# One gate and one product per tile, with hand-counted semaphores in one critical section (SwiGLU, 8192 x 8192, fp32)

## Chip, cores and metric

One core of one Trainium2 chip. The metric is the device time of one execution in microseconds (us). "Span" is the length of the profiled execution, which is about 1.8 us shorter than the timed one. A transfer "lands" when its completion is signalled (the packet records put that about 0.3 us before the semaphores do), and "stands in line" while an earlier transfer of its queue is still under way. A packet is one piece of a transfer in the DMA records.

## The reference

```python
def reference(x):                      # x: 8192 x 8192 float32
    a, b = np.split(x, 2, axis=-1)
    return a * (b / (1 + np.exp(-b)))  # 8192 x 4096
```

Each element is read once and each result written once: 268.4 MB in, 134.2 MB out, hardly any arithmetic.

## The kernel before

A tile holds two rows of x on each of 128 partitions (64 KB each); there are 32 tiles and three buffers. Loads go out from the sync engine, the first 30 stores from GpSimd, the last three (tile 30, and the two halves of tile 31) again from the sync engine. The framework derives all waits.

```python
    def swiglu(i, k, c0=0, cw=half):               # one row k of tile i
        xt = tiles[i]
        b = xt[:, k * M + half + c0 : k * M + half + c0 + cw]
        nc.scalar.activation(out=b, in_=b, func=_SILU)
        nc.vector.tensor_mul(out=xt[:, k * half + c0 : ...], in0=xt[:, k * M + c0 : ...], in1=b)   # (cut)

    for i in range(BUFS):
        load(i)
    for i in range(last):                          # last = 31
        for k in range(R):                         # R = 2
            swiglu(i, k)
        if i == last - 1:
            swiglu(last, 0)
        store(i)
        ...                                        # load(i + 3); tile 31 in two halves
    store(last, 0, half)
    for c0 in range(0, half, half // 2):
        swiglu(last, 1, c0, half // 2)
    store(last, half, half)
```

## Time and profile before

| | before |
|---|---|
| time, median | 936.34 us in the first three runs, 935.93 in the six that stand beside the change |
| span of the profiled run | 934.3 us |
| DMA share of the two data queues | 99.8% |
| first data packet / end of the last one (packet records of the trace) | 1.76 us / 932.76 us |
| busy: vector engine, scalar engine | 30%, 25% |

The lines behind the shares are in the prediction, and so is what follows from them. This is the list of instructions of the framework's last line; columns are the queue, the instruction, its count, duration in ns (least, median, most), and first and last start:

```profile
L106 POOLq DRAIN  x3: 40/101/32876, 871.2 to 934.0; - x3
```

GpSimd's queue (POOL) begins a drain at 871.2 us, right after issuing its last store, and it lasts 32.9 us, until 904.1. The last GpSimd store has landed at 902.5 by the packet records. So this drain, an instruction that holds GpSimd's queue, ended 1.6 us after the last of its stores had landed, and it lies wholly beside other transfers.

### The profile page before, as it was taken

How to read it: one execution, taken by the hardware profiler on the slowest of the kernel's cores; microseconds unless marked ns; L12 is line 12 of the kernel's file. 1: busy time of each engine (PE TensorE's matmuls, PEld its weight loads, DVE VectorE, ACT ScalarE, POOL GpSimd, SP SyncE). 2: the span in 40 equal slices, each digit the busy share in tenths (PEclk: the TensorE clock that was granted, in tenths of full speed). 3: DMA queues.
4: the chain of work that ended last, by engine and by line, in shares of the span. 5: the costliest groups of instructions: out<-in, count | busy, mean ns of one | idle time of the engine just before them, and what ended most of it. 6: DMA issues, size and time to landing. Idle time of an engine off the chain costs nothing.

```text
span 934.3 us, 400 instructions
## 1 busy us (share of the span) xinstructions
DVE 283.3 (30%) x65; ACT 229.4 (25%) x66; POOL 16.3 (2%) x34
## 2 busy tenths in 40 slices
DVE  0333312333113332133321333213333133331252
ACT  0323330233311333113331133311333203332041
POOL 0000000000000000000000000000000000000000
DMA  9999999999999999999999999999999999999998
GB/s 404 404 449 426 425 448 424 436 429 446 428 422 441 432 446 424 446 415 453 428 421 456 415 452 421 427 450 415 442 428 441 429 435 428 438 450 414 437 432 383
DMA packets 9507, 402.68 MB, mean 431 GB/s; under 512 B 1056, under 2 KB 1056, under 8 KB 1056
## 3 DMA queue, kind: packets, MB, share of 16 engines
q1 hardware_dynamic: 5184, 276.83, 68.6%
q0 software_dynamic: 4320, 125.83, 31.2%
q14 instruction: 3, 0.02, 0.0%
HBM read 268.44 MB, written 134.22 MB: 431 GB/s over the span
## 4 chain that ended last, share of the span: by engine, by line
DMA 84%; DVE 10%; ACT 4%; issue 1%; DVEq 0%; SPq 0%; ACTq 0%
DMA out_dram<-xt 43%; DMA xt<-in_x_dram 40%; DVE xt L51 10%; ACT xt L50 4%; DVEq L106 0%; SPq L43 0%; ACTq L50 0%; DVEq L51 0%
## 5 line engine op out<-in xcount | busy, mean ns | idle before, releaser
L51 DVE TENSOR_TENSOR xt<-xt 128x4096 f32<-128x4096 f32 (+1 forms) x65 | 283.3, 4359 | 636.9 <-ACT xt L50 633.7
L50 ACT ACTIVATE xt<-xt 128x4096 f32<-128x4096 f32 (+1 forms) x65 | 228.1, 3556 | 687.3 <-DMA xt<-in_x_dram 687.3
L58 POOL DMA_DIRECT2D out_dram<-xt x30 | 16.1, 537 | 854.8 <-DVE xt L51 854.8
L50 ACT ACT_TABLE_LOAD x1 | 1.3, 1283 | 0.7 <-PEq L95 0.7
L95 POOL MEMSET const-float32-0.0<- 128x1 f32 x1 | 0.1, 99 | 0.2 <-issue 0.2
L95 POOL MEMSET const-bfloat16-1.0<- 128x1 bf16 x1 | 0.1, 102 | 0.0
L95 POOL MEMSET const-float32-1.0<- 128x1 f32 x1 | 0.1, 99 | 0.0
L95 POOL MEMSET const-uint8-127<- 128x1 uint8 x1 | 0.1, 99 | 0.0
## 6 DMA issues: line engine op xcount, KB each, us to landing
out_dram<-xt POOLq DMA_DIRECT2D x30, 4096.0 KB, 40.5
xt<-in_x_dram SPq DMA_DIRECT2D x2, 4096.0 KB, 26.4
out_dram<-xt SPq DMA_DIRECT2D x1, 4096.0 KB, 23.8
out_dram<-xt SPq DMA_DIRECT2D x2, 2048.0 KB, 14.5
xt<-in_x_dram SPq DMA_DIRECT2D x31, 33.5
```

The source lines that it names most:

```text
L50: nc.scalar.activation(out=b, in_=b, func=_SILU)
L51: nc.vector.tensor_mul(out=xt[:, k * half + c0 : k * half + c0 + cw], in0=xt[:, k * M + c0 : k * M + c0 + cw], in1=b,)
L58: (nc.gpsimd if i < last - 1 else nc.sync).dma_start(out=ov[i * P : (i + 1) * P, c0 : c0 + cw], in_=tiles[i][:, c0 : c0 + cw])
L95: nc = _bacc.Bacc("TRN2", target_bir_lowering=False, num_devices=1)
```

## The change

The intent is to have fewer instructions and no derived waits: one gate and one product per tile (tiles 1 to 30), and semaphores counted by hand, inside one critical section (a stretch of the program into which the framework puts no waits of its own). Cut to its core:

```diff
-    pool = ctx.enter_context(tc.tile_pool(name="sbuf", bufs=BUFS))
-    ctx.enter_context(tc.manual_schedule())
+    slots = [pool.tile([P, R * M], x.dtype, name=f"slot{s}") for s in range(BUFS)]
+    load_sem, store_sem = ...   # one per slot; and last_sem, gate_sem, prod_sem, end_sem
     def load(i, ...):
+        if i >= BUFS:
+            nc.sync.wait_ge(store_sem[s], 16 * (i // BUFS))
         nc.sync.dma_start(...)
+            .then_inc(last_sem if c0 else load_sem[s], 16)
     def swiglu(i, k0=0, k1=R, c0=0, cw=half):      # rows k0..k1 in one access pattern
+        nc.scalar.wait_ge(load_sem[s], 16 * (i // BUFS + 1))
         nc.scalar.activation(out=b, in_=b, func=_SILU).then_inc(gate_sem, 1)
+        nc.vector.wait_ge(gate_sem, counts["gate"])
         nc.vector.tensor_mul(...).then_inc(prod_sem, 1)
     def store(i, eng, ...):
+        eng.wait_ge(prod_sem, counts["prod"])
         inst = eng.dma_start(...)                   # then_inc(store_sem[s]) or, last three, end_sem
-    ... loop
+    with tc.tile_critical():
+        ... the same loop; tile 0 still in two rows
+        if i == last - 1:
+            swiglu(last, 0, 1)                     # counted before ...
+        store(i, ...)                              # ... the store of tile 30 is written
+        nc.sync.wait_ge(store_sem[(last - 2) % BUFS], 16 * ((last - 2) // BUFS + 1))
+        nc.sync.wait_ge(end_sem, 16 * counts["end"])
```

More of the change, by code (lines that the diff above doesn't have):

```diff
@@ L33 @@
     last = ntiles - 1
-    pool = ctx.enter_context(tc.tile_pool(name="sbuf", bufs=BUFS))
-    ctx.enter_context(tc.manual_schedule())
-    tiles = {}
-    def load(i, rows=None):
-        if i not in tiles:
-            tiles[i] = pool.tile([P, R * M], x.dtype, name="xt")
-        lo, hi = (0, R) if rows is None else rows
-        nc.sync.dma_start(
-            out=tiles[i][:, lo * M : hi * M], in_=xv[i * P : (i + 1) * P, lo * M : hi * M]
-        )
-    def swiglu(i, k, c0=0, cw=half):
-        xt = tiles[i]
-        b = xt[:, k * M + half + c0 : k * M + half + c0 + cw]
-        nc.scalar.activation(out=b, in_=b, func=_SILU)
-        nc.vector.tensor_mul(
-            out=xt[:, k * half + c0 : k * half + c0 + cw],
-            in0=xt[:, k * M + c0 : k * M + c0 + cw],
-            in1=b,
-        )
@@ L57, in store @@
-    def store(i, c0=0, cw=R * half):
-        (nc.gpsimd if i < last - 1 else nc.sync).dma_start(
-            out=ov[i * P : (i + 1) * P, c0 : c0 + cw], in_=tiles[i][:, c0 : c0 + cw]
-        )
-    for i in range(BUFS):
-        load(i)
-    for i in range(last):
-        for k in range(R):
-            swiglu(i, k)
-        if i == last - 1:
-            swiglu(last, 0)
-        store(i)
-        nxt = i + BUFS
-        if nxt < last:
-            load(nxt)
-        elif nxt == last:
-            load(last, (0, 1))
-            load(last, (1, 2))
@@ L77 @@
-    store(last, 0, half)
-    for c0 in range(0, half, half // 2):
-        swiglu(last, 1, c0, half // 2)
-    store(last, half, half)
+    pool = ctx.enter_context(tc.tile_pool(name="sbuf", bufs=1))
+    slots = [pool.tile([P, R * M], x.dtype, name=f"slot{s}") for s in range(BUFS)]
+    load_sem = [tc.alloc_semaphore(f"load{s}") for s in range(BUFS)]
+    store_sem = [tc.alloc_semaphore(f"store{s}") for s in range(BUFS)]
+    last_sem = tc.alloc_semaphore("last")
+    gate_sem = tc.alloc_semaphore("gate")
@@ new lines, with load, rows @@
+    prod_sem = tc.alloc_semaphore("prod")
+    end_sem = tc.alloc_semaphore("end")
+    def load(i, c0=0, cw=R * M):
+        s = i % BUFS
+        if i >= BUFS:
+            nc.sync.wait_ge(store_sem[s], 16 * (i // BUFS))
+        nc.sync.dma_start(
+            out=slots[s][:, c0 : c0 + cw], in_=xv[i * P : (i + 1) * P, c0 : c0 + cw]
+        ).then_inc(last_sem if c0 else load_sem[s], 16)
+    counts = {"gate": 0, "prod": 0, "end": 0}
+    def rows(ap, k0, k1, pitch, c0, cw):
+        return ap[:, k0 * pitch : k1 * pitch].rearrange("p (r w) -> p r w", w=pitch)[
+            :, :, c0 : c0 + cw
+        ]
@@ new lines, in swiglu @@
+    def swiglu(i, k0=0, k1=R, c0=0, cw=half):
+        s = i % BUFS
+        xt = slots[s]
+        b = rows(xt, k0, k1, M, half + c0, cw)
+        if i == last and k0:
+            nc.scalar.wait_ge(last_sem, 16)
+        else:
+            nc.scalar.wait_ge(load_sem[s], 16 * (i // BUFS + 1))
+        nc.scalar.activation(out=b, in_=b, func=_SILU).then_inc(gate_sem, 1)
+        counts["gate"] += 1
+        if k0:
+            nc.vector.wait_ge(prod_sem, counts["prod"])
+        nc.vector.wait_ge(gate_sem, counts["gate"])
+        nc.vector.tensor_mul(
+            out=rows(xt, k0, k1, half, c0, cw), in0=rows(xt, k0, k1, M, c0, cw), in1=b
+        ).then_inc(prod_sem, 1)
+        counts["prod"] += 1
@@ new lines, in store @@
+    def store(i, eng, c0=0, cw=R * half):
+        s = i % BUFS
+        eng.wait_ge(prod_sem, counts["prod"])
+        inst = eng.dma_start(
+            out=ov[i * P : (i + 1) * P, c0 : c0 + cw], in_=slots[s][:, c0 : c0 + cw]
+        )
+        if i < last - 1:
+            inst.then_inc(store_sem[s], 16)
+        else:
+            inst.then_inc(end_sem, 16)
+            counts["end"] += 1
+    with tc.tile_critical():
+        for i in range(BUFS):
+            load(i)
+        for i in range(last):
+            if i == 0:
+                for k in range(R):
+                    swiglu(i, k, k + 1)
+            else:
+                swiglu(i)
+            if i == last - 1:
+                swiglu(last, 0, 1)
+            store(i, nc.gpsimd if i < last - 1 else nc.sync)
+            nxt = i + BUFS
+            if nxt < last:
+                load(nxt)
+            elif nxt == last:
+                load(last, 0, M)
+                load(last, M, M)
+        store(last, nc.sync, 0, half)
+        for c0 in range(0, half, half // 2):
+            swiglu(last, 1, 2, c0, half // 2)
+        store(last, nc.sync, half, half)
+        nc.sync.wait_ge(store_sem[(last - 2) % BUFS], 16 * ((last - 2) // BUFS + 1))
+        nc.sync.wait_ge(end_sem, 16 * counts["end"])
```

## The prediction

> **What bounds the kernel now.** I read the page first, then the chain that ended last, then the timeline of one stretch in the middle and of the end, and last the waits of the sync engine's queue. The page gives the bound at once:
>
> ```profile
> DVE 283.3 (30%) x65; ACT 229.4 (25%) x66; POOL 16.3 (2%) x34
> ...
> DMA  9999999999999999999999999999999999999998
> ...
> q1 hardware_dynamic: 5184, 276.83, 68.6%
> q0 software_dynamic: 4320, 125.83, 31.2%
> ...
> HBM read 268.44 MB, written 134.22 MB: 431 GB/s over the span
> ```
>
> The two queues' packets fill 68.6 + 31.2 = 99.8% of what 16 DMA engines have in 934.3 us, while no compute engine is busy above 30%. Whatever a change does to the vector and scalar engines can reach the time only if it opens a hole in this DMA work. (The hardware queue q1 carries the loads and the last three stores, all issued by the sync engine; the software queue q0 carries the first 30 stores, issued by GpSimd.)
>
> How near is this to what the DMA can do? The chain shows the steady rate, because it walks round one buffer: load, gate, products, store, next load into the same buffer.
>
> ```profile
> 447.05 0.02 SPq L43
> 447.07 0.03 issue
> 447.11 33.62 DMA xt<-in_x_dram
> 480.75 0.04 ACTq L50
> 480.79 0.05 issue
> 480.83 3.62 ACT xt L50
> 484.46 0.02 issue
> 484.48 4.44 DVE xt L51
> 488.92 0.03 issue
> 488.97 0.04 issue
> 489.01 4.44 DVE xt L51
> 493.45 0.28 issue
> 493.73 40.56 DMA out_dram<-xt
> 534.29 0.02 SPq L43
> ```
>
> One turn takes 534.29 - 447.05 = 87.24 us here; over eight turns (186.00 to 882.21 in the same view) it is 87.03 us. Three buffers turn in it, so one tile takes 29.01 us. A tile moves 8.389 MB in and 4.194 MB out, 12.583 MB: 433.8 GB/s. At that rate the whole 402.65 MB takes 928.2 us, so only 934.3 - 928.2 = 6.1 us of the span is anything but full-speed transfer: issue and start of the first load, and the last landing and closing barrier.
>
> The chain looks like a latency chain ("DMA 84%, DVE 10%, ACT 4%"), and a reader could conclude that DVE's 10% can be bought back, or that a longer product is paid every turn. That is the trap of this view. Whether a step of the turn matters depends on whether the transfer after it finds the queue empty. The timeline tells:
>
> ```profile
> 422.74 7.12 ACT L50 ACTIVATE xt<-xt 128x4096 f32<-128x4096 f32 x2 [21.98 <-DMA xt<-in_x_dram]
> 426.39 8.95 DVE L51 TENSOR_TENSOR xt<-xt 128x4096 f32<-128x4096 f32 x2 [20.15 <-ACT xt L50]
> 435.64 0.53 POOL L58 DMA_DIRECT2D out_dram<-xt  x1 [28.57 <-DVE xt L51]
> 451.74 7.12 ACT L50 ACTIVATE xt<-xt 128x4096 f32<-128x4096 f32 x2 [21.88 <-DMA xt<-in_x_dram]
> ```
>
> This store is issued at 435.64, but the store before it (issued at 406.54) lands only at 447.05: it waits behind it for 11.4 us. Likewise the load issued at 447.11 finds the load before it unfinished until 451.74: 4.6 us. So both queues always hold work, with 11.4 + 4.6 = 16.0 us of standing in line per turn.
>
> **What the Trainium skill says.** "DMA: Bandwidth & Descriptors", section Specifications, gives a fabric ceiling of 435 GB/s for the 16 engines; the trace's 433.8 GB/s is that ceiling, so no new order of waits can raise the rate. The same page, section Issuing engines are not separate DMA queues, says that transfers issued from different engines run on the same 16 engines and interleave; the trace agrees (99.8% is the sum of q0 and q1), so time one queue leaves is taken by the other. "ScalarE: Activation LUTs", section What ACT_TABLE_LOAD costs, gives 186 ns + 0.833 ns per element for an activation with immediates; the trace has 3616 ns for 4096 elements and 1901 ns (a mean of two) for 2048, a slope of 0.837 and about 190 ns fixed. "VectorE: DVE Perf Modes", section Mode 1×, has one result a cycle as the mode that fp32 falls back to; 4425 and 2288 ns give 1.043 ns per element (1/0.96 GHz is 1.042) and about 150 ns fixed.
>
> **The change, part by part.** The bytes, the transfers' shapes, the engines that issue them and the three buffers are unchanged.
>
> (1) One gate and one product of 2 x 4096 columns per tile, for tiles 1 to 30. By the two fits the gate is 0.19 + 8192 x 0.837 = 7.05 us, the product 0.15 + 8192 x 1.0435 = 8.70 us. Before, the second gate ran beside the first product. So landing to store issue goes from 12.9 us (480.83 to 493.73) to 7.05 + 8.70 + about 0.3 for the hand-offs = 16.05 us: +3.1 us per tile. Busy time falls: 30 x 0.15 = 4.5 us of DVE and 30 x 0.19 = 5.7 us of ACT at most, both off the path. The 3.1 us comes out of the store's 11.4 us in line, leaving about 8.3 us. The store lands when it did, so the next load is issued when it was. Cost: 0.
>
> (2) Tile-made waits become one wait per instruction. A sequencer's step costs 0.02 to 0.05 us in the chain; a dozen saved per turn would be half a microsecond of latency, again absorbed by the line. Gain: 0.
>
> (3) The first tile is still split in two: first store as before at 35.6 us. Cost 0. The second store moves from 57.66 to about 60.8; the first store was issued at 35.63 and has 34.4 us to landing, 70.0, so it still queues. Cost 0.
>
> (4) The end. The store of tile 30 now waits on the one shared product counter at its value after the first half of tile 31, since that product is counted before the store is written. Before:
>
> ```profile
> 899.64 20.89 SPq L58 DMA_DIRECT2D out_dram<-xt  x3
> 904.11 3.62 ACT L50 ACTIVATE xt<-xt 128x4096 f32<-128x4096 f32 x1 [9.97 <-DMA xt<-in_x_dram]
> 907.75 4.43 DVE L51 TENSOR_TENSOR xt<-xt 128x4096 f32<-128x4096 f32 x1 [8.14 <-ACT xt L50]
> 913.73 3.71 ACT L50 ACTIVATE xt<-xt 128x2048 f32<-128x2048 f32 x2 [6.01 <-DMA xt<-in_x_dram]
> ```
>
> So it goes out not at 899.64 but at 907.75 + 4.43 = 912.2, 12.5 us later. But it is in the sync engine's queue, behind the last half load, which lands at 913.7; until then the engines have that load to move. The first load of the kernel is issued at 0.74, and its first data packet starts at 2.5 in the raw record: 1.8 us. So the store's packets would start at about 914.0 instead of directly at 913.7: a hole of about 0.3 us, up to 1 us on engines that finish early. From there 8.4 MB of stores (one tile, two halves of the last) keep the engines busy: 19.3 us at 433.8 GB/s, to 933. The last product is issued for storing near 920, well before its turn. Cost: +0.3 to +1.
>
> (5) Entry to and exit from the critical section, and two waits at the end in place of the list of ten at line 106. The record does not show the new form. Before, the last bytes land near 933.2 and the span ends at 934.3. I allow -0.3 to +0.6.
>
> Sum: 936.34 + 0.4 (the hole, a little above its central figure) + 0.1 (entry and exit) = 936.8 us.
>
> **Rivals.** *The longer latency is paid each turn.* If nothing stood in line, 87.03 would become 90.1 us, 1.03 us per tile, and 29 tiles make +30 us: 966 us, slower by 3%. For it: every step is in the chain, and a gate and a product that no longer overlap are the one real loss here. Against: 16 us in line, and 99.8% DMA share. Even a drained store queue would only hand its time to the loads. *The late store of tile 30 opens a full hole.* If the engines had nothing to do from 899.6 to 912.2 it would cost 12.5 us: 949 us, still within 2%. Against: the load landing at 913.7, in the same queue. *Fewer waits and instructions make it faster.* At best it recovers all non-transfer time, 6.1 us or 0.65%: 930 us. Faster by 2% would take 917 us, below the 928.2 that the bytes need. *The critical section serialises the engines.* If its waits held issues back in program order, or loads ahead of their buffers were lost, the DMA share would fall and tens of microseconds could appear. Against: the waits in the diff are per engine and per slot, and loads keep their distance of three tiles.
>
> **Range and chances.** The bulk is pinned by bytes and rate; what can move is the end and the entry, some tenths of a microsecond to two. Run-to-run spread is 935.99 to 936.64. So 936.8, 8 in 10 within 935.5 to 938.6. Faster by 2% is excluded by the bytes (0.5%); slower by 2% needs the first or the last rival (1.5%).
>
> **What would show it.** Right: DMA share still above 99%, turns of 87.0 us; ACT about 7.0 and DVE about 8.7 us for a tile, not overlapping; store issue-to-landing down from 40.5 to about 37.4 us; load landing still about 33.5; the store of tile 30 issued near 912 and at most 1 us of idle DMA there. Wrong: turns near 90 us or DMA share in the nineties' lower half mean that the line was no slack; a hole of several microseconds near 900 to 914 means that the end was misread; a product much above 8.7 us means that the two-row access pattern has a cost of its own.

## The result, and the profile after

Time after: 938.45 us median (938.27 to 938.65, six runs), beside 935.93 us before (935.80 to 936.64, six runs). Ratio 1.0025, 95% interval 1.0013 to 1.0038: within 2%, but a real loss of 2.5 us. (A ratio is the mean time of one kernel's fast runs over that of the other's of the same rounds, so not quite the ratio of the medians quoted.)

The page after, four of the lines shown in the prediction:

```profile
DVE 278.6 (30%) x35; ACT 226.6 (24%) x36; POOL 16.3 (2%) x34
...
DMA  9999999999999999999999999999999999999997
...
q1 hardware_dynamic: 5184, 276.83, 68.4%
q0 software_dynamic: 4320, 125.83, 31.1%
```

The DMA share is 99.5% of a span that is 2.4 us longer. The chain of waits after, the turn that stands against the one shown before (start, duration, what):

```profile
446.90 33.81 DMA slot<-in_x_dram
480.71 0.02 issue
480.74 7.04 ACT slot L67
487.78 0.02 issue
487.80 8.70 DVE slot L72
496.50 0.28 issue
496.79 37.28 DMA out_dram<-slot
534.06 0.02 issue
534.08 33.55 DMA slot<-in_x_dram
```

The turn is 87.18 us here (446.90 to 534.08), before 87.24; over eight turns (185.88 to 882.08 in the same view) it is 87.0 us, as before. Gate and product no longer overlap, and landing to store issue grew from 12.9 to 16.05 us. The store's time to landing shrank from 40.56 to 37.28 us: the store is issued later and lands at the same moment.

So the 2.5 us are not in the loop. The timeline at the end shows the late store of tile 30:

```profile
907.52 4.43 DVE L72 TENSOR_TENSOR slot<-slot 128x4096 f32<-128x4096 f32 x1 [5.04 <-ACT slot L67]
911.97 8.61 SPq L80 DMA_DIRECT2D out_dram<-slot  x3
```

It goes out at 911.97, before at 899.64. The idle time of the DMA engines between 912 and 916 us, from the packet records, is 0.13 us on average (4 us less a sixteenth of the time that packets took in them; before: none). The last data ends at 932.64 us, even 0.12 us earlier than before.

What is new comes after that. The list of the critical section's own instructions, and the waits of the sync engine's queue (us in total, times, longest):

```profile
L89 POOLq DRAIN  x1: 2506/2506/2506, 933.3 to 933.3; - x1
```

```profile
SPq L89 <- POOLq L89: 2.3, 1, 2.3
```

Once the sync engine has passed its two end waits, at 933.1 us, the engines that took part in the section drain. The scalar and vector engines' drains take 0.01 us. GpSimd's takes 2.506 us, from 933.3 to 935.8, with nothing left to move, and the sync engine waits 2.3 us for it. The account of the 2.38 us of span (936.66 - 934.28), with times in us from the packet records:

| | before | after | difference |
|---|---|---|---|
| start to first data packet | 1.76 | 1.96 | +0.20 |
| first to last data | 931.01 | 930.68 | -0.33 |
| last data to end of span | 1.52 | 4.03 | +2.51 |

### The profile page after: what moved, and what is told of

It is laid out like the page before. It is cut to its first block, busy times and chain, and to the rows that moved or that the text cites. A ratio compares the mean times of both kernels' runs of the same rounds, so it can differ in the third digit from the quotient of the medians.

```text
span 936.7 us, 196 instructions
## 1 busy us (share of the span) xinstructions
DVE 278.6 (30%) x35; ACT 226.6 (24%) x36; POOL 16.3 (2%) x34
## 4 chain that ended last, share of the span: by engine, by line
DMA 80%; DVE 10%; ACT 8%; issue 0%; SPq 0%; DVEq 0%
DMA out_dram<-slot 40%; DMA slot<-in_x_dram 40%; DVE slot L72 10%; ACT slot L67 8%; SPq L48 0%; SPq L138 0%; DVEq L71 0%; SPq L89 0%
## 5 line engine op out<-in xcount | busy, mean ns | idle before, releaser
L72 DVE TENSOR_TENSOR slot<-slot 128x8192 f32<-128x8192 f32 (+2 forms) x35 | 278.6, 7960 | 641.6 <-ACT slot L67 641.5
L67 ACT ACTIVATE slot<-slot 128x8192 f32<-128x8192 f32 (+2 forms) x35 | 225.3, 6443 | 689.8 <-DMA slot<-in_x_dram 689.8
L80 POOL DMA_DIRECT2D out_dram<-slot x30 | 16.1, 536 | 857.8 <-DVE slot L72 857.8
## 6 DMA issues: line engine op xcount, KB each, us to landing
out_dram<-slot POOLq DMA_DIRECT2D x30, 4096.0 KB, 37.4
```

What stands on the lines that cost most here:

```text
L67: nc.scalar.activation(out=b, in_=b, func=_SILU).then_inc(gate_sem, 1)
L72: nc.vector.tensor_mul(out=rows(xt, k0, k1, half, c0, cw), in0=rows(xt, k0, k1, M, c0, cw), in1=b).then_inc(prod_sem, 1)
L80: inst = eng.dma_start(out=ov[i * P : (i + 1) * P, c0 : c0 + cw], in_=slots[s][:, c0 : c0 + cw])
```

## The experiments

My theory: the loss is GpSimd's drain. Before, it stands right behind GpSimd's last store and is hidden; in the critical section it starts only when the sync engine has finished, and it is exposed. Rival A: leaving a section costs GpSimd 2.5 us whatever went before. Rival B: the longer gate and product, or the late store, cost the time. "After" in this part is the changed kernel; unless it says otherwise, a diff starts from it. The diffs are shortened, and words in parentheses stand for code. Every run was correct.

**An explicit drain, early**

```diff
             store(i, nc.gpsimd if i < last - 1 else nc.sync)
+            if i == last - 2:
+                nc.gpsimd.drain()
```

> The changed kernel with one explicit drain added on GpSimd right after its last store (issued near 874 us, far from the end). Theory: the 2.5 us that the change added beyond the forecast is GpSimd's drain on leaving the critical section, which takes 2.51 us at 933.3 us, after the last byte has landed, because no drain of GpSimd's software transfers has been done before; the kernel before has its long drain at 871.2 us beside the transfers. Then this one is 2.4 to 2.5 us faster than the changed kernel, 936.0 us, ratio to before 1.000, and GpSimd's drain on leaving takes about 0.1 us or less. Rival A (a drain of GpSimd at the section's end costs 2.5 us whatever came before): no change, 938.4 us. Rival B (the longer gate and product, or the late store of tile 30, cost the time): no change, 938.4 us.

936.32 us (935.99 to 936.43), ratio to before 1.0002. The two drains:

```profile
L89 POOLq DRAIN  x1: 41/41/41, 933.5 to 933.5; - x1
```

```profile
L102 POOLq DRAIN  x1: 29552/29552/29552, 874.3 to 874.3; - x1
```

The early drain takes 29.6 us beside the transfers, until 903.8. The one on leaving the section, at the same place as after, now takes 0.041 us. Rivals A and B both fall: nothing else was touched, and 2.1 us came back. I had expected 2.4 to 2.5. In the profile, the time from the last data to the end of the span fell from 4.03 to 1.74 us, but the last data ended 0.26 us later (932.89), and 0.30 us of idle engines stood between 912 and 916, where after had 0.13.

**The end waits in a section of their own**

```diff
+    with tc.tile_critical():
         nc.sync.wait_ge(store_sem[(last - 2) % BUFS], ...)
         nc.sync.wait_ge(end_sem, ...)
```

> The changed kernel with its two end waits moved out of the critical section into a second critical section that holds nothing else. Theory: the handshake on leaving the first section, with GpSimd's 2.5 us drain, then starts when the sync engine has issued its last store, near 921 us, and runs beside the last stores; 936.0 to 936.3 us. Rival A (a drain of GpSimd costs 2.5 us wherever it stands, and the final barrier has one more): 938.4 us or more. Rival B (gate, product, late store): 938.4 us.

936.07 us (935.84 to 936.29), ratio to before 1.0000.

```profile
L89 POOLq DRAIN  x1: 2506/2506/2506, 920.6 to 920.6; - x1
```

The same drain, of the same length, but at 920.6, beside the last stores. Here its price is unchanged and only its place is: it costs nothing that these runs can tell. (The plainer form, the two waits behind the section with no section of their own, did not build: the framework reported a deadlock. So there is no run of it.)

**The store of tile 30 with its exact count**

```diff
+            done = counts["prod"]
             if i == last - 1:
                 swiglu(last, 0, 1)
-            store(i, ...)
+            store(i, ..., done=done)               # waits for done
```

> The changed kernel with the store of tile 30 waiting for its own product's count, not for the next one's; it should go out near 902.5 us instead of 912.0. Theory: the late store costs what the trace shows as idle engine time there, 0.1 us, so 938.3 us, ratio to the changed kernel within 0.0003. Rival (the late store is the loss): 936 us, 2 us or more faster.

938.34 us (938.17 to 938.61), ratio to before 1.0025, the same as the changed kernel's.

```profile
902.39 18.10 SPq L80 DMA_DIRECT2D out_dram<-slot  x3
```

The store goes out 9.6 us earlier, and the last data ends at 932.55 instead of 932.64. The engines are not idle between 912 and 916 here. In this pair of profiles the late store is worth about 0.1 us; the run with split rows shows that it can be more.

**Two gates and two products per tile in the critical section**

```diff
-            if i == 0: (two rows)   else: swiglu(i)
+            for k in range(R):
+                swiglu(i, k, k + 1)
```

> The changed kernel with two gates and two products per tile, as before. Theory: the longer latency is taken from the time that stores stand in line and costs nothing, so 938.4 us, within 0.2 us of the changed kernel; store issue to landing back at about 40.5 us. Rival (one gate and one product lengthen the run): 936 us.

938.72 us (938.63 to 939.65), ratio to before 1.0031: 0.3 us slower than the changed kernel, not faster. A store takes 39.8 us to landing (expected: about 40.5). Splitting does not recover anything. I had expected a difference within 0.2 us. The intervals of the two ratios overlap (1.0018 to 1.0043, and 1.0013 to 1.0038). But the profiled run is the slowest of the five (939.65 us); in it the engines were idle for 0.96 us between 912 and 916, beside the late store of tile 30, and the last data ended at 933.86. So the late store is the likely cause in that run; the other four left no profile.

**The merging alone, in the kernel before**

```diff
-        for k in range(R):
-            swiglu(i, k)
+        if i == 0: (two rows)   else: whole(i)    # one activation and one tensor_mul over both rows
```

> The kernel before with one gate and one product per tile for tiles 1 to 30, and nothing else of the change. Theory: nothing to gain or lose, 936.0 us, within 0.3 us of the kernel before; store issue to landing from 40.5 to about 37.4 us. Rival (the merging is what lost 2.5 us): 938.4 us.

935.98 us (935.85 to 936.13), ratio to before 1.0000. The stores' issues on the page:

```profile
out_dram<-xt POOLq DMA_DIRECT2D x30, 4096.0 KB, 37.0
```

The third number is the median from issue to landing, 40.5 us before. The merging is free: the store is issued later by 3.1 us and takes 3.5 us less to land, so it is paid from time in line.

**The early stores on the scalar engine**

```diff
-            store(i, nc.gpsimd if i < last - 1 else nc.sync)
+            store(i, nc.scalar if i < last - 1 else nc.sync)
```

> The changed kernel with the first 30 stores issued by the scalar engine, so that GpSimd issues no transfer at all. Theory: GpSimd's drain on leaving the section costs 2.5 us because of the software transfers it has issued; here it takes 0.1 us or less and the run ends near 936.0 us. Rival A (leaving a section costs GpSimd 2.5 us in any case): drain of 2.5 us and 938.4 us. Rival C (stores in the hardware queue change the shares of loads and stores): a time well off both.

936.78 us (936.25 to 937.47), ratio to before 1.0008, interval 0.9996 to 1.0021. GpSimd has now no part in the section at all, and its longest drain is 0.18 us, at the start. The drain's cost is gone; that the section asks for no drain at all makes this run weaker evidence against rival A than the first one. The last data ends later here (933.35 us), so part of what was won is lost: 0.75 us of idle engines stand between 912 and 916, beside the late store again. Why that hole is larger here stays open.

**One GpSimd store only**

```diff
+            store(i, nc.gpsimd if i == 0 else nc.scalar if i < last - 1 else nc.sync)   # own semaphore for tile 0
```

> As the kernel with all early stores on the scalar engine, but the store of the first tile is issued by GpSimd, near 36 us; nothing else is in its queue. If the 2.5 us is a fixed price of the first drain after a software transfer: 2.5 us and 938.4 us. If it goes by the number of transfers since the last drain (30 gave 2.506 us, so 0.08 us each): about 0.1 us and 936.0 us.

936.27 us (936.14 to 936.89), ratio to before 1.0004.

```profile
L93 POOLq DRAIN  x1: 135/135/135, 933.3 to 933.3; - x1
```

The drain took 0.135 us. So it is no fixed price; it goes by the number of software transfers (those that GpSimd issues), or by how long ago they were.

**The kernel before, with GpSimd held until the end**

```diff
     store(last, half, half)
+    nc.gpsimd.memset(tiles[last][:, half : half + 1], 0.0)   # must wait for the last store
```

> The kernel before, with one small memset on GpSimd at the end that must wait for the last store, so that its drain can only start after the last byte has landed. No critical section. Theory: the price goes with the place of the drain and not with the section: the drain takes 2.5 us (or the rest of it) at 933 us and the time is 938.4 to 938.8 us. Rival A (the section's own handshake costs it): 936.0 to 936.4 us.

938.33 us (938.07 to 938.48), ratio to before 1.0024.

```profile
L107 POOLq DRAIN  x3: 40/99/2651, 933.1 to 936.3; - x3
```

This is the counterpart: no critical section, no merged work, no counted semaphores, and the loss of the change appears in full when GpSimd's drain is pushed to 933.1 us. There it takes 2.65 us, and the time from the last data to the end of the span is 4.01 us, against 1.52 before. The memset itself takes 0.10 us.

**Ten GpSimd stores out of 30**

```diff
+            store(i, nc.sync if i >= last - 1 else nc.scalar if i % BUFS else nc.gpsimd)
```

> The changed kernel with ten of the first 30 stores (every third tile) issued by GpSimd and twenty by the scalar engine. If the drain goes by the number of transfers since the last drain, the line through one transfer (0.135 us) and thirty (2.506 us) gives 0.053 + 0.082 x 10 = 0.87 us for GpSimd's drain on leaving the section, and about 936.9 us. If one transfer was cheap only because it was issued 897 us before, and any recent transfer costs the whole price, the drain takes 2.5 us and the time is 938.5 us.

936.86 us (936.69 to 936.91, four runs), ratio to before 1.0009.

```profile
L89 POOLq DRAIN  x1: 877/877/877, 933.3 to 933.3; - x1
```

The line through one and thirty forecast 0.87 us; it took 0.877.

**A drain after the 20th store**

```diff
+            if i == 19:
+                nc.gpsimd.drain()
```

> The changed kernel with one explicit drain on GpSimd after its 20th store, so that ten stores come between it and the drain on leaving the section. If the drain goes by the transfers since the last drain: 0.87 us at the end, span 1.6 us shorter than the changed kernel's, 936.8 us. If it goes by all transfers since the start: 2.5 us, 938.4 us. The explicit drain waits until its last store has landed, so the next store goes out up to 9 us late, against about 8.3 us in line: the transfers should lose nothing, at most a few tenths.

940.03 us (939.72 to 941.73), ratio to before 1.0048: half right. The drains:

```profile
L89 POOLq DRAIN  x1: 871/871/871, 936.4 to 936.4; - x1
```

```profile
L102 POOLq DRAIN  x1: 38062/38062/38062, 583.9 to 583.9; - x1
```

The drain at the end took 0.871 us, as for ten transfers: what counts is the transfers since the last drain, not all of them and not their age. But I expected 936.8 us, with nothing lost in the middle, and the transfers took 933.8 us instead of 930.7. The drain held GpSimd until 622.0, so the store of tile 20 went out at 622.50 instead of about 612.9 (its product ended at 612.65), 9.6 us late. The store before it landed at 621.1 by its semaphore, so in time it would have stood in line for 8.2 us. The packet records show the store queue dry from about 620 to 628: the first packet of this store started at 628.4, 5.9 us after its issue. The engines were idle for no more than 0.06 us there, as forecast for a dry queue. Yet from 620 to 632 the packets took 1.2 us longer than their usual durations (1.8 us longer over the whole run than in the changed kernel), and the late store of tile 30 left 1.2 us of idle engines between 912 and 916, where the changed kernel had 0.13. I think that the phase of loads and stores had shifted; no run tests this. The size of the time in line was right, but it is not all slack: the lead-in from issue to first packet has to fit into it as well. That fits what the record shows: running past its end was dearer than I had said.

GpSimd's drain when nothing is outstanding any more, all runs together:

| software transfers since its last drain | drain, us | run |
|---|---|---|
| 0 | 0.041 | explicit drain, early |
| 1 | 0.135 | one GpSimd store |
| 10 | 0.877 and 0.871 | ten GpSimd stores; drain after the 20th |
| 30 | 2.506 (2.651 at the framework's own closing) | after, and three experiments; kernel before with GpSimd held |

From 1 to 30 that is (2.506 - 0.135) / 29 = 0.082 us per transfer. Each of these transfers is a store of 4096 KB from 128 partitions; whether the price goes by transfers or by their descriptors was not separated. A drain that begins while stores are outstanding ends when they have landed and a little later: 1.6 us after the last of 30 (before; explicit drain, early), 1.2 us after the last of 20 (drain after the 20th).

The late store of tile 30 has its own list. The idle time of the engines between 912 and 916, one profiled run each, was 0.07 us with two sections, 0.10 with ten GpSimd stores, 0.13 in the changed kernel, 0.19 with one GpSimd store, 0.30 with the early drain, 0.75 with the early stores on the scalar engine, 0.96 with split rows and 1.22 with the drain after the 20th. The four kernels that issue this store early (before, exact count, merging alone, GpSimd held until the end) have none. What sets the size of the hole was not tested.

No version is clearly faster than the kernel before. The best of the changed ones, with two sections, equals it.

## Why the prediction was right or wrong

The time, 938.45 us, lies in the range of 935.5 to 938.6, near its upper edge, and the outcome is "within 2%", which had 98%. The central 936.8 was 1.65 us too low, and beside the 935.93 of the same rounds the change cost 2.5 us where 0.5 was stated. Nearly all of that is one term. That the time still lies in the range is owed to the range's margin and not to the mechanism: the sum's own upper allowances, +1 for the end and +0.6 for entry and exit, reach only 937.9.

- **The bound and the room below it: right.** The DMA engines set the time before and after; the turn of a buffer went from 87.24 to 87.18 us, 87.0 over eight turns in both, as stated.
- **(1) One gate and product, cost 0: right, and shown twice.** Gate 7.03 and product 8.69 us against 7.05 and 8.70; landing to store issue 16.05; store to landing 37.4 us, as stated. The merging alone in the kernel before changed nothing (1.0000), and splitting again in the changed kernel gained nothing.
- **(2) Fewer waits, gain 0: right.** The changed kernel has 204 fewer recorded instructions (400 to 196); with two sections, where the drain is hidden, it takes what the kernel before takes (1.0000).
- **(3) The first tile: right.** The second store was issued at 60.69 us, and the store of tile 0 had not landed.
- **(4) The late store of tile 30, +0.3 to +1: the mechanism right, the size too high for the changed kernel.** It went out at 911.97, as stated, but left only 0.13 us idle, and its exact count gained 0.1 us. In three experiments the hole was 0.75 to 1.22 us. I also misread the record here: its clock and the profile's differ by about 0.75 us. The first data packet starts at 1.76 us, so issue to packet is 1.0 us and not 1.8. This fits the smaller hole.
- **(5) Entry and exit, "I allow -0.3 to +0.6": the step that failed.** Entry cost 0.20 us. The exit cost 2.51 us, nearly all of it GpSimd's drain: with the early drain, which leaves 0.041 us of it there, the exit costs only 1.74 - 1.52 = 0.22 us. "The record does not show the new form" was true of the section but not of the drain: the 32.9 us line stood in the profile of before and should have made me ask what a drain waits for, and who would wait for it if it came last. I did not ask.
- **The rivals.** Latency paid each turn: refuted. Full hole of 12.5 us: refuted. Faster by up to 6 us: refuted. The fourth, a section that serialises the engines, came nearest: the sync engine did wait for another engine, but only at the section's exit and only for GpSimd. One sentence of the rivals was too strong, that a drained store queue "would only hand its time to the loads": when it ran dry (drain after the 20th store), the engines stayed busy, but their packets took 1.2 us longer.

Two figures of the Trainium skill agree with the traces: "DMA: Bandwidth & Descriptors", section Specifications, with 435 GB/s against 433.8, and "ScalarE: Activation LUTs", section What ACT_TABLE_LOAD costs, with 186 ns + 0.833 ns per element, from which an estimate for the merged gate is 7.01 us, against 7.03 measured.

## What to carry to other kernels

Where the transfers are the bound, first measure how long each transfer stands in line in its own queue. Engine latency well below that time was free here (3.1 of 11.4 us), and in the one run that went past it, it cost more than its excess. The lead-in of a transfer (5.9 us there) also has to fit into the line. Then account for what comes after the last byte, since nothing hides there: keep GpSimd's drain out of it, by draining right behind its last software transfer or by letting the section end before the last waits. A wait moved to one common end made the closing work of every engine in the section start at the latest moment here, even that of GpSimd, which had long been done.

## What the Trainium skill lacked or had wrong

- "DMA: Bandwidth & Descriptors", section SWDGE vs HWDGE vs iDMA: no price is given for a drain of GpSimd after software transfers. The runs show 0.04 us with none since the last drain, 0.135 with one, 0.87 with ten, 2.51 with thirty, all with the data long landed.
- "VectorE: DVE Perf Modes", section The DRAIN you can't avoid, puts the drains that the runtime adds around a kernel at about 12 ns on all five engines. The drains here carry lines of the kernel, so they need not be the ones meant, but a reader could take that size for them. After the change, those of the framework's closing took 7 to 10 ns on the scalar, vector, tensor and sync engines and 34 to 96 ns on GpSimd; where GpSimd's came last with 30 transfers behind it, it took 2.65 us (kernel before with GpSimd held). No page has this.
- "DMA: Bandwidth & Descriptors", section Where 436 GB/s comes from, says that for transfers between HBM and SBUF the HBM side (about 358 GB/s) binds. With one core running, 433.8 GB/s were sustained here, reads and writes together, so the sentence lacks a condition. The same page supplies it elsewhere: its own measurements, up to 425 GB/s, are of one core with the other idle.
- The same page, section Specifications, gives about 1 us to the first byte for GpSimd's transfers. Into engines already full of loads it took 6.5 us (kernel before, store of tile 0, issued at 35.6, first packet at 42.2), and a store issued by the scalar engine there fared little better (issued at 35.5, first packet at 39.7, second at 42.5).
